# Matmul operand read as two half-rows in turn in a one-core decoder layer

## The chip, the core and the metric

One NeuronCore of a Trainium2 chip runs the whole kernel. The metric is the device time of one execution in microseconds (us), the median of the runs shown. The engines are named as in the profile: PE is TensorE, PEld its weight loads, DVE is VectorE, ACT is ScalarE, POOL is GpSimd, SP is SyncE, which issues most of the DMAs.

## The reference

The kernel computes one layer of a decoder for 256 prompt tokens and 32 sample tokens (8 sequences of 4), 2048 features wide, in float32. Cut to what matters here, with the attention and the convolutions named and not shown:

```python
z = einsum('ntd,de->nte', x, w_in)
h, gate_b, gate_c, q, k, v, g_a, g_b = split(z)
ya = gate_b * causal_conv3(gate_c * h)          # mixer A
yb = dilated_window_attention(q, k, v)          # mixer B, 3 groups of 4 heads
mixed = sigmoid(g_a) * (ya @ w_branch_a) + sigmoid(g_b) * (yb @ w_branch_b)
x1 = layernorm(ALPHA * x + mixed @ w_out)
a, b = split(x1 @ w_up)                         # 2048 -> 2 x 5632
y = layernorm(ALPHA * x1 + (silu(causal_conv3(a)) * b) @ w_down)
```

## The kernel before

Features lie on the 128 partitions and the T = 288 tokens (256 prompt, then 32 sample) lie along the free axis. An activation is a tile of KD = 16 rows per partition, one row of 288 float32 values for each block of 128 features. The activations of the layer's input stand in `xh` and `xl`; the other products read `yah`/`yal`, `ybh`/`ybl` (in later stages the names are reused for the mixed sum and the gated FFN values).

Every matrix product is made in float32r, a float32 form that PE takes in one pass, with three matmuls for one block of weights: each operand is split into a rounded high part and a low rest (`split`, `half_block`), and high times high, high times low and low times high are added up in PSUM. `mms` (lines 170 to 181) issues these three matmuls for each of the rows `k`: weights `hi[:, c, :]` (128x128) against the row `xh[:, k]`, the same weights against `xl[:, k]`, then `lo[:, c, :]` against `xh[:, k]`. A product over 16 rows is so 48 matmuls, each with its own weight load, into one PSUM tile `acc` of 288 columns; five such tiles are in use in turn.

`product` (line 157) takes the next prepared weights from `w_ready`, has `prepare` load (SP queue, tile `wst`, 1 MB) and split (ACT line 120, DVE line 121) the block after it, and calls `mms`. The stages follow each other: 12 products for q, 24 for k and v with the prompt's attention between them, 48 for mixer A, 64 for the two gated branches, 16 for `w_out`, then three parts of the FFN with 2 x 16, 2 x 16 and 2 x 12 products of `w_up`, each followed by 16 of `w_down`. The sample attention is woven in as steps between products of the early stages (its matmuls are lines 323 and 373).

In the first part of the FFN the normalisation is not applied to `x` before the product. Two columns more, the norm's scale and shift (`TG` = 290 columns), go through the same matmuls, and `normed` (line 581) puts the result right afterwards: it copies the two columns to a small tile `wgb` and corrects the 288 others with `n1.r` and `n1.nmr`. For this `xh` and `xl` have rows of `TX` = 296 values (1184 bytes); all other activations have rows of 288 (1152 bytes).

What leaves PSUM is read by ACT or DVE: `act.copy` of q, k, v and h, the sigmoids (lines 476, 487), `gated` (line 441), the products with `pc` (lines 461, 462), the sums into `dd` (lines 567, 573, 631, 635), `normed` (line 586) and the copies to `u` (lines 606, 607). POOL works on SBUF alone. The instruction order on each engine is the scheduler's, made when the program is built.

Of the kernel before, what the change touches and what calls it, by code (L numbers as in the profile page):

```python
# [11 lines left out]
F32R = mybir.dt.float32r  # L12
# [5 lines left out]
P = 128  # L18
# [4 lines left out]
NS = NB * NT  # L23
T = SEQ + NS

TG = T + 2
TX = T + 8
FF = 5632
KF = FF // P
HK = KD // 2  # L30
# [41 lines left out]
def layer_kernel(ctx: ExitStack, tc: tile.TileContext, ins, outs):  # L72
# [14 lines left out]
    def sb(pl, shape, tag, dt=F32, bufs=None):  # L87
        return pl.tile(shape, dt, tag=tag, name=nm(tag), bufs=bufs)

    def acc(cols=T):  # L90
        return sb(ps, [P, cols], "acc")

    def att(cols=512):
        return sb(ps, [P, cols], "att", bufs=2)
# [1 line left out]
    def f32(ap):  # L96
        return ap.bitcast(F32)
# [56 lines left out]
            copy_rest(d)  # L154
        w_ready.append([half_block(st, k0, min(HK, nk - k0)) for k0 in range(0, nk, HK)])

    def product(x, cols=T):

        w = w_ready.pop(0)
        if not w_ready:  # L160
            prepare()
        if steps_on[0]:
            spent[0] += N_STEP
            while spent[0] >= N_STEP_BLOCKS:
                spent[0] -= N_STEP_BLOCKS
                next(steps, None)
        o = acc(cols)
        mms(o, w, x)
        return o

    def mms(out, w, x):
        xh, xl = x
        nk = sum(n for _, _, n in w)
        k = 0
        for hi, lo, n in w:
            for c in range(n):
                n_cols = out.shape[-1]
                pe.matmul(out, hi[:, c, :], xh[:, k, :n_cols], start=k == 0, stop=False)  # L178
                pe.matmul(out, hi[:, c, :], xl[:, k, :n_cols], start=False, stop=False)  # L179
                pe.matmul(out, lo[:, c, :], xh[:, k, :n_cols], start=False, stop=k == nk - 1)  # L180
                k += 1

    def split(hi, lo, src):
        act.copy(hi, src)  # L184
        dve.tensor_tensor(lo, src, f32(hi), ALU.subtract)  # L185
# [4 lines left out]
    pool.memset(ones_p, 1.0 / P)  # L190


    xh = sb(big, [P, KD, TX], "xh", F32R)
    xl = sb(big, [P, KD, TX], "xl", F32R)
    x_in = ins["x"].rearrange("p (k t) -> p k t", t=T)
    xs = sb(big, [P, KD, T], "yah")
    w_ready = []
# [5 lines left out]
    for k0, n in FIRST:  # L203
        k = slice(k0, k0 + n)
        h = slice(k0 % HK, k0 % HK + n)
        for b, (st, src) in enumerate(stage):
            sp.dma_start(st[:, k, :], src[:, k, :])
            if b == 0:
                sp.dma_start(xs[:, k, :], x_in[:, k, :])
            hi, lo, _ = w_ready[b][k0 // HK]  # L210
            act.copy(hi[:, h, :], st[:, k, :])
            dve.tensor_tensor(lo[:, h, :], st[:, k, :], f32(hi[:, h, :]), ALU.subtract)
            if b == 0:
                split(xh[:, k, :T], xl[:, k, :T], xs[:, k, :])
    x = (xh, xl)

    cst = sb(big, [P, C_M0], "cst")

# [178 lines left out]
    kv = sb(big, [P, 2, 2, NG, T], "dd")  # L397
    for j in range(NH):
        for g in range(NG):
            act.copy(q_all[:, j, g], product(x))  # L400
            if j == 0 and g > 0:
                for dst, src in ((cst, ins["cst"][:, :C_M0]), (m_dist, ins["cst"][:, C_M0:])) if g == 1 else ((prm, ins["prm"]),):
                    behind(sp.dma_start(dst, src), w_load[0])
        pool.tensor_copy(q_s[:, :, j, :], q_all[:, j, :, SEQ:])
    steps_on[0] = True
    for j in range(NH):
        kT, vT = (kv[:, j % 2, c] for c in range(2))
        for g in range(NG):
            for t in (kT, vT):
                act.copy(t[:, g, :], product(x))  # L410
        pool.tensor_copy(k_s[:, :, j, :], kT[:, :, SEQ:])
        pool.tensor_copy(v_s[:, j], vT[:, :, SEQ:])
        act.dma_start(outs["o_k"][j].rearrange("p (g t) -> p g t", g=NG), kT)
        act.dma_start(outs["o_v"][j].rearrange("p (g t) -> p g t", g=NG), vT)
        prompt_attention(j, q_all[:, j], kT, vT)
# [16 lines left out]
    def samples(t):  # L432
        return t[:, SEQ:].rearrange("p (b r) -> p b r", b=NB)

    def last_rows(dst, u):
        pool.tensor_copy(dst[:, 0:2], u[:, SEQ : SEQ + 2])  # L436
        return pool.tensor_copy(
            dst[:, 2:].rearrange("p (b r) -> p b r", b=NB),
            u[:, SEQ + 2 :].rearrange("p (b r) -> p b r", b=NB)[:, :, NT:],
        )  # L440

    def gated(out, y, o, add=None):

        yt = y[:, SEQ : SEQ + NB * (NT + 2)].rearrange("p (b r) -> p b r", b=NB)
        for a, b, c in ((out[:, :SEQ], y[:, :SEQ], o[:, :SEQ]), (samples(out), yt[:, :, 2:], samples(o))):
            if add is None:
                dve.tensor_tensor(a, b, c, ALU.mult)  # L447
            else:
                dve.scalar_tensor_tensor(a, c, add, b, ALU.add, ALU.mult)

    yah = sb(big, [P, KD, T], "yah", F32R)
# [2 lines left out]
    for i in range(KD):  # L454
        ph = product(x)
        h = sb(wk, [P, T], "h", bufs=2)
        act.copy(h, ph)
        pc = product(x)
        u = sb(wk, [P, UW + 2], "u", bufs=2)
        up, us = conv_in(u[:, :UW], R_SM + i * 2 * NB)  # L460
        dve.tensor_tensor(up, h[:, :SEQ], pc[:, :SEQ], ALU.mult)  # L461
        dve.tensor_tensor(us, samples(h), samples(pc), ALU.mult)
        last_rows(cm[:, i], u[:, :UW])
        y = conv(u, R_WCM + i * 3)
        pb = product(x)
        ya = sb(wk, [P, T], "ya", bufs=2)
        gated(ya, y, pb)
        split(yah[:, i], yal[:, i], ya)
# [4 lines left out]
    for i in range(KD):  # L473
        pg = product(x)
        sg = sb(wk, [P, T], "h", bufs=2)
        act.activation(sg, pg, AF.Sigmoid)
        o = product((yah, yal))
        dve.tensor_tensor(ma[:, i], sg, o, ALU.mult)
    for _ in steps:
        pass  # L480
    steps_on[0] = False
# [2 lines left out]
    for i in range(KD):  # L484
        pg = product(x)
        sg = sb(wk, [P, T], "h", bufs=2)
        act.activation(sg, pg, AF.Sigmoid)
        o = product((ybh, ybl))
        m = sb(wk, [P, T], "ya", bufs=2)
        dve.tensor_tensor(m, sg, o, ALU.mult)  # L490
        pool.tensor_tensor(m, m, ma[:, i], ALU.add)  # L491
        split(mxh[:, i], mxl[:, i], m)

# [66 lines left out]

    n1 = Norm(R_LN, R_LN + KD)
    for i in range(KD):
        o = product((mxh, mxl))
        xf = sb(wk, [P, T], "h", bufs=2)
        pool.tensor_tensor(xf, f32(xh[:, i, :T]), f32(xl[:, i, :T]), ALU.add)
        if i == 0:
            dve.scalar_tensor_tensor(dd[:, i], xf, ALPHA, o, ALU.mult, ALU.add)
            n1.first()
            for c in range(2):
                split(xh[:, :, T + c], xl[:, :, T + c], prm[:, R_LN + c * KD : R_LN + (c + 1) * KD])  # L570
        else:
            dve.scalar_tensor_tensor(xf, xf, ALPHA, n1.c, ALU.mult, ALU.subtract)
            dve.tensor_tensor(dd[:, i], xf, o, ALU.add)  # L573
        act.activation(xh[:, i, :T], dd[:, i], AF.Copy, scale=n1.at(n1.g, i))
        dve.scalar_tensor_tensor(
            xl[:, i, :T], dd[:, i], n1.at(n1.g, i), f32(xh[:, i, :T]), ALU.mult, ALU.subtract
        )
        n1.add(i)
    n1.finish(False)

    def normed(o):

        w = sb(wk, [P, 2], "wgb", bufs=4)
        act.copy(w, o[:, T:])
        t = sb(wk, [P, T], "h", bufs=2)
        dve.tensor_tensor(t, o[:, :T], n1.r, ALU.mult)
        dve.scalar_tensor_tensor(t, n1.nmr, w[:, 0:1], t, ALU.mult, ALU.add)
        return t, w[:, 1:2]

# [4 lines left out]
    for part, nf in enumerate(THIRDS):  # L594
        gh = sb(big, [P, KD, T], "yah", F32R)
        gl = sb(big, [P, KD, T], "yal", F32R)
        for k in range(nf):
            pa = product(x, TG if part == 0 else T)
            u = sb(wk, [P, UW + 2], "u", bufs=2)
            up, us = conv_in(u[:, :UW], R_SF + f * 2 * NB)  # L600
            if part == 0:
                pa, b1 = normed(pa)
                act.activation(up, pa[:, :SEQ], AF.Identity, bias=b1)
                act.activation(us, samples(pa), AF.Identity, bias=b1)
            else:
                act.copy(up, pa[:, :SEQ])  # L606
                act.copy(us, samples(pa))
            i_rows = last_rows(cf[:, f], u[:, :UW])
            y = conv(u, R_WCF + f * 3)
            act.activation(y, y, AF.Silu)  # L610
            pb = product(x, TG if part == 0 else T)
            gf = sb(wk, [P, T], "ya", bufs=2)
            if part == 0:
                gated(gf, y, *normed(pb))
# [10 lines left out]
        if f == KF:  # L625
            sp.dma_start(outs["o_cf"].rearrange("p (k r) -> p k r", k=KF), cf)
        for i in range(KD):
            o = product((gh, gl))
            if part == 0:
                split(xh[:, i, :T], xl[:, i, :T], dd[:, i])  # L630
                dve.scalar_tensor_tensor(dd[:, i], dd[:, i], ALPHA, o, ALU.mult, ALU.add)
            else:
                if f == KF and i > 0:
                    pool.tensor_tensor(dd[:, i], dd[:, i], n2.c, ALU.subtract)
                dve.tensor_tensor(dd[:, i], dd[:, i], o, ALU.add)
            if f == KF:
                if i == 0:
                    n2.first()
                n2.add(i)
# [192 lines left out]
```

## Time and profile before

| what | value |
|---|---|
| median of 3 runs | 1914.95 us (1914.68 to 1915.04) |
| the profiled execution: its own time | 1915.33 us |
| its span in the trace | 1913.6 us |
| matmul records | 14257, of them 13632 in float32r into `acc` |
| granted PE clock, mean | 0.996 |
| DVE, ACT, POOL busy | 1009.6, 799.7, 257.6 us |
| HBM read, written | 389.89 MB, 94.53 MB |

The profile gives for each group of instructions the line, the engine, the tiles (out<-in), the shape, the count, the busy time and the mean length of one. Matmuls are pipelined: the length of one in the trace, some 0.3 us, runs past the start of the next. What counts for the time is the step from one start to the next, which is read from the timeline (start, length, what) or from a stretch of time divided by the number of matmuls in it (the windows: stretch, its length, then busy us and count for each engine).

### The profile page before, as it was taken

The numbers are of one execution on the slowest core, as the hardware profiler recorded it, in microseconds if no ns is written. First come the engines' busy times: TensorE is split into PE (matmuls) and PEld (weight loads), VectorE is DVE, ScalarE is ACT, GpSimd is POOL, SyncE is SP. The second block draws the span as 40 slices with busy tenths as digits, with TensorE's granted clock in tenths as the row PEclk, the third lists the DMA queues.
The fourth block names the chain that finished last, engine by engine and source line by source line (L and its number), as shares of the span: only waits on it lengthen the run. The fifth ranks groups of instructions, "written<-read, shape, count | busy, mean of one in ns | idle before, by whom it ended". The sixth has DMA issues, their size and how long they took to land.

```text
span 1913.6 us, 33492 instructions
## 1 busy us (share of the span) xinstructions
PE 1885.7 (99%) x14257; PEld 1848.0 (97%) x14257; DVE 1009.6 (53%) x1270; ACT 799.7 (42%) x1153; POOL 257.6 (13%) x406
## 2 busy tenths in 40 slices
PE   8999999999999999999999999999999999999995
PEld 8999999999999999999999999999999999999995
DVE  4444445445444433445587777764455554455555
ACT  4334443333333333344444555553444443344444
POOL 0000000000000000001154233310011100011174
PEclk9999999999999999999999999999999999999998
DMA  7586766777777777566755555556555555555552
GB/s 290 203 286 245 261 241 245 279 256 269 269 257 266 277 255 280 170 237 237 258 210 213 203 201 204 215 200 219 201 218 205 214 209 210 213 206 217 214 185 81
DMA packets 59862, 436.25 MB, mean 228 GB/s; under 512 B 7232, under 2 KB 7616, under 8 KB 15680
## 3 DMA queue, kind: packets, MB, share of 16 engines
q1 hardware_dynamic: 58560, 430.58, 62.3%
q10 hardware_dynamic: 1152, 3.54, 0.5%
q8 instruction: 111, 1.82, 0.4%
q14 instruction: 39, 0.32, 0.0%
HBM read 389.89 MB, written 94.53 MB: 253 GB/s over the span
## 4 chain that ended last, share of the span: by engine, by line
PE 98%; DVE 1%; ACT 0%; DMA 0%; ACTq 0%; SPq 0%; issue 0%
PE acc L178 32%; PE acc L180 32%; PE acc L179 31%; PE long L323 1%; PE long L373 1%; PE att L259 0%; PE att L278 0%; ACT yah L645 0%; DMA yah<-in_x 0%; DVE dd L543 0%; PE att L274 0%; DVE dd L557 0%; PE att L252 0%; PE att L529 0%; PE att L530 0%; DVE xl L185 0%
## 5 line engine op out<-in xcount | busy, mean ns | idle before, releaser
L121 DVE TENSOR_TENSOR wlo<-wst,whi 128x1024 fp32r<-128x1024 f32 (+1 forms) x580 | 706.3, 1219 | 713.6 <-ACT whi L120 700.8
L120 ACT CAST whi<-wst 128x1024 fp32r<-128x1024 f32 (+1 forms) x580 | 594.0, 1025 | 1004.0 <-PE acc L179 891.7
L178 PE MATMUL acc<-xh,whi 128*128 128x288 f32 (+1 forms) x3264 | 970.5, 298 | 7.4 <-ACT xh L184 7.4
L179 PE MATMUL acc<-xl,whi 128*128 128x288 f32 (+1 forms) x3264 | 966.8, 296 | 0.3 <-DVE xl L185 0.3
L180 PE MATMUL acc<-xh,wlo 128*128 128x288 f32 (+1 forms) x3264 | 967.1, 296 | 0.0
L178 PEld LDWEIGHTS acc<-xh,whi 128*128 128x128 f32 x3264 | 615.8, 189 | 28.1 <-issue 19.9
L180 PEld LDWEIGHTS acc<-xh,wlo 128*128 128x128 f32 x3264 | 616.2, 189 | 1.1 <-issue 0.8
L179 PEld LDWEIGHTS acc<-xl,whi 128*128 128x128 f32 x3264 | 615.6, 189 | 1.1 <-DVE xl L185 0.6
L180 PE MATMUL acc<-yah,wlo 128*128 128x288 f32 x1216 | 359.6, 296 | 0.0
L178 PE MATMUL acc<-yah,whi 128*128 128x288 f32 x1216 | 359.4, 296 | 0.0
L179 PE MATMUL acc<-yal,whi 128*128 128x288 f32 x1216 | 356.9, 294 | 0.0
L178 PEld LDWEIGHTS acc<-yah,whi 128*128 128x128 f32 x1216 | 228.6, 188 | 4.3 <-issue 4.2
L179 PEld LDWEIGHTS acc<-yal,whi 128*128 128x128 f32 x1216 | 228.6, 188 | 0.1
L180 PEld LDWEIGHTS acc<-yah,wlo 128*128 128x128 f32 x1216 | 228.3, 188 | 0.1
L436 POOL COPY qk_s<-u 128x2 f32<-128x2 f32 x44 | 43.5, 988 | 630.1 <-ACT u L606 480.4
L429 DVE SCALAR_TENSOR_TENSOR cy<-u,prm,cy 128x304 f32<-128x304 f32 x120 | 70.8, 590 | 3.1 <-ACT cy L427 0.3
L491 POOL TENSOR_TENSOR ya<-ya,dd 128x288 f32<-128x288 f32 x16 | 13.9, 868 | 332.8 <-DVE ya L490 332.8
L447 DVE TENSOR_TENSOR ya<-cy,acc 128x256 f32<-128x256 f32 x88 | 23.0, 301 | 44.1 <-PE acc L180 44.1
L436 POOL COPY cm<-u 128x2 f32<-128x2 f32 x16 | 3.0, 185 | 281.5 <-DVE u L461 281.5
L184 ACT CAST yah<-ya 128x288 fp32r<-128x288 f32 x76 | 32.7, 431 | 10.8 <-POOL ya L491 9.4
L185 DVE TENSOR_TENSOR yal<-ya,yah 128x288 fp32r<-128x288 f32 x76 | 35.0, 461 | 1.2 <-ACT yah L184 1.2
L521 POOL TENSOR_TENSOR cache<-cache,dd 128x288 f32<-128x288 f32 x28 | 26.8, 958 | 56.8 <-DVE dd L573 37.5
(146 smaller groups left out, 804.4 us busy)
## 6 DMA issues: line engine op xcount, KB each, us to landing
wst<-in_w_in SPq DMA_DIRECT2D x114, 1024.0 KB, 5.2
wst<-in_w_up SPq DMA_DIRECT2D x88, 1024.0 KB, 4.8
wst<-in_w_down SPq DMA_DIRECT2D x32, 1024.0 KB, 4.8
cache<-in_ck SPq DMA_DIRECT2D x18, 1024.0 KB, 6.9
out_o_ck<-cache SPq DMA_DIRECT2D x18, 1024.0 KB, 7.7
cache<-in_cv SPq DMA_DIRECT2D x18, 1024.0 KB, 7.0
out_o_cv<-cache SPq DMA_DIRECT2D x18, 1024.0 KB, 8.5
wst<-in_w_a SPq DMA_DIRECT2D x16, 1024.0 KB, 6.2
```

Source lines behind the costliest of these rows:

```text
L120: act.copy(hi[:, :n, :], st[:, k0 : k0 + n, :])
L121: dve.tensor_tensor(lo[:, :n, :], st[:, k0 : k0 + n, :], f32(hi[:, :n, :]), ALU.subtract)
L178: pe.matmul(out, hi[:, c, :], xh[:, k, :n_cols], start=k == 0, stop=False)
L179: pe.matmul(out, hi[:, c, :], xl[:, k, :n_cols], start=False, stop=False)
L180: pe.matmul(out, lo[:, c, :], xh[:, k, :n_cols], start=False, stop=k == nk - 1)
L184: act.copy(hi, src)
L185: dve.tensor_tensor(lo, src, f32(hi), ALU.subtract)
L323: pe.matmul(p[j * NS : (j + 1) * NS], qm[:, j, b, :], c[:, o + j * cols : o + (j + 1) * cols], start=b == 0, stop=b == NB - 1,)
L429: dve.scalar_tensor_tensor(y, u[:, i : i + YW], prm[:, w0 + i : w0 + i + 1], y, ALU.mult, ALU.add)
L436: pool.tensor_copy(dst[:, 0:2], u[:, SEQ : SEQ + 2])
L447: dve.tensor_tensor(a, b, c, ALU.mult)
L521: pool.tensor_tensor(self.s1, self.s1, d, ALU.add)
```

## The change

`xh` and `xl` get the shape [128, 16, 2, 160]: each row of 288 tokens is stored as two halves of 144 which start 160 values (640 bytes) apart, so a row takes 1280 bytes. The two columns for the norm become one more column in each half. The other activations keep their rows of 288 and are only seen as two halves of 144 (576 bytes apart).

The matmul reads its moving operand as column 0 of the first half, column 0 of the second, column 1 of the first, and so on. Its output is written in that order to consecutive PSUM columns, and whoever reads PSUM reads every second column to get a half back. Where the prompt's 256 columns were read alone they are now two pieces, 144 and 112, so that there are two instructions in place of one. The tile `wgb` gets two buffers in place of four. The core of the diff:

```diff
-TG = T + 2
-TX = T + 8
+H = T // 2
+HG = H + 1
+HX = 160
...
-    def acc(cols=T):
-        return sb(ps, [P, cols], "acc")
+    def acc(half=H):
+        return sb(ps, [P, half, 2], "acc")
+
+    def h2(ap):
+        return ap.rearrange("p (h a) -> p h a", h=2)
+
+    def h3(ap):
+        return ap.rearrange("p k (h a) -> p k h a", h=2)
...
-        o = acc(cols)
+        o = acc(x[0].shape[-1])
         mms(o, w, x)
-        return o
+        return o.rearrange("p a h -> p h a")
...
-                n_cols = out.shape[-1]
-                pe.matmul(out, hi[:, c, :], xh[:, k, :n_cols], start=k == 0, stop=False)
-                pe.matmul(out, hi[:, c, :], xl[:, k, :n_cols], start=False, stop=False)
-                pe.matmul(out, lo[:, c, :], xh[:, k, :n_cols], start=False, stop=k == nk - 1)
+                xh_k, xl_k = (t[:, k].rearrange("p h a -> p a h") for t in x)
+                pe.matmul(out, hi[:, c, :], xh_k, start=k == 0, stop=False)
+                pe.matmul(out, hi[:, c, :], xl_k, start=False, stop=False)
+                pe.matmul(out, lo[:, c, :], xh_k, start=False, stop=k == nk - 1)
...
-    xh = sb(big, [P, KD, TX], "xh", F32R)
-    xl = sb(big, [P, KD, TX], "xl", F32R)
+    xh = sb(big, [P, KD, 2, HX], "xh", F32R)
+    xl = sb(big, [P, KD, 2, HX], "xl", F32R)
...
-    x = (xh, xl)
+    x = (xh[:, :, :, :H], xl[:, :, :, :H])
+    x_gb = (xh[:, :, :, :HG], xl[:, :, :, :HG])
...
+    def pieces(up, us):
+
+        return up[:, :H], up[:, H:SEQ], us
+
+    def from_psum(o):
+        return o[:, 0], o[:, 1, : SEQ - H], o[:, 1, SEQ - H :].rearrange("p (b r) -> p b r", b=NB)
...
-        dve.tensor_tensor(up, h[:, :SEQ], pc[:, :SEQ], ALU.mult)
-        dve.tensor_tensor(us, samples(h), samples(pc), ALU.mult)
+        for a, b, c in zip(pieces(up, us), pieces(h, samples(h)), from_psum(pc)):
+            dve.tensor_tensor(a, b, c, ALU.mult)
...
-        o = product((yah, yal))
-        dve.tensor_tensor(ma[:, i], sg, o, ALU.mult)
+        o = product((h3(yah), h3(yal)))
+        dve.tensor_tensor(h2(ma[:, i]), h2(sg), o, ALU.mult)
...
-        w = sb(wk, [P, 2], "wgb", bufs=4)
-        act.copy(w, o[:, T:])
+        w = sb(wk, [P, 2], "wgb", bufs=2)
+        act.copy(w, o[:, :, H])
...
-                act.copy(up, pa[:, :SEQ])
-                act.copy(us, samples(pa))
+                for a, b in zip(pieces(up, us), from_psum(pa)):
+                    act.copy(a, b)
```

More of the change, by code (lines that the diff above doesn't have):

```diff
@@ L155, in prepare, with product @@
         w_ready.append([half_block(st, k0, min(HK, nk - k0)) for k0 in range(0, nk, HK)])
-    def product(x, cols=T):
+    def product(x):
         w = w_ready.pop(0)
@@ L166, in product @@
                 next(steps, None)
-        o = acc(cols)
+        o = acc(x[0].shape[-1])
         mms(o, w, x)
-        return o
+        return o.rearrange("p a h -> p h a")
     def mms(out, w, x):
-        xh, xl = x
         nk = sum(n for _, _, n in w)
@@ L213, in layer_kernel @@
             if b == 0:
-                split(xh[:, k, :T], xl[:, k, :T], xs[:, k, :])
-    x = (xh, xl)
+                split(xh[:, k, :, :H], xl[:, k, :, :H], h3(xs[:, k]))
+    x = (xh[:, :, :, :H], xl[:, :, :, :H])
+    x_gb = (xh[:, :, :, :HG], xl[:, :, :, :HG])
     cst = sb(big, [P, C_M0], "cst")
@@ L399, in layer_kernel @@
         for g in range(NG):
-            act.copy(q_all[:, j, g], product(x))
+            act.copy(h2(q_all[:, j, g]), product(x))
             if j == 0 and g > 0:
@@ L409, in layer_kernel @@
             for t in (kT, vT):
-                act.copy(t[:, g, :], product(x))
+                act.copy(h2(t[:, g, :]), product(x))
         pool.tensor_copy(k_s[:, :, j, :], kT[:, :, SEQ:])
@@ L444, in gated @@
         yt = y[:, SEQ : SEQ + NB * (NT + 2)].rearrange("p (b r) -> p b r", b=NB)
-        for a, b, c in ((out[:, :SEQ], y[:, :SEQ], o[:, :SEQ]), (samples(out), yt[:, :, 2:], samples(o))):
-            if add is None:
+        if add is None:
+            for a, b, c in zip(pieces(out, samples(out)), pieces(y, yt[:, :, 2:]), from_psum(o)):
                 dve.tensor_tensor(a, b, c, ALU.mult)
-            else:
+        else:
+            for a, b, c in ((out[:, :SEQ], y[:, :SEQ], o[:, :SEQ]), (samples(out), yt[:, :, 2:], samples(o))):
                 dve.scalar_tensor_tensor(a, c, add, b, ALU.add, ALU.mult)
@@ L456, in layer_kernel @@
         h = sb(wk, [P, T], "h", bufs=2)
-        act.copy(h, ph)
+        act.copy(h2(h), ph)
         pc = product(x)
@@ L475, in layer_kernel @@
         sg = sb(wk, [P, T], "h", bufs=2)
-        act.activation(sg, pg, AF.Sigmoid)
-        o = product((yah, yal))
-        dve.tensor_tensor(ma[:, i], sg, o, ALU.mult)
+        act.activation(h2(sg), pg, AF.Sigmoid)
+        o = product((h3(yah), h3(yal)))
+        dve.tensor_tensor(h2(ma[:, i]), h2(sg), o, ALU.mult)
     for _ in steps:
@@ L486, in layer_kernel @@
         sg = sb(wk, [P, T], "h", bufs=2)
-        act.activation(sg, pg, AF.Sigmoid)
-        o = product((ybh, ybl))
+        act.activation(h2(sg), pg, AF.Sigmoid)
+        o = product((h3(ybh), h3(ybl)))
         m = sb(wk, [P, T], "ya", bufs=2)
-        dve.tensor_tensor(m, sg, o, ALU.mult)
+        dve.tensor_tensor(h2(m), h2(sg), o, ALU.mult)
         pool.tensor_tensor(m, m, ma[:, i], ALU.add)
@@ L562, in layer_kernel @@
     for i in range(KD):
-        o = product((mxh, mxl))
+        o = product((h3(mxh), h3(mxl)))
         xf = sb(wk, [P, T], "h", bufs=2)
-        pool.tensor_tensor(xf, f32(xh[:, i, :T]), f32(xl[:, i, :T]), ALU.add)
+        pool.tensor_tensor(h2(xf), f32(x[0][:, i]), f32(x[1][:, i]), ALU.add)
         if i == 0:
-            dve.scalar_tensor_tensor(dd[:, i], xf, ALPHA, o, ALU.mult, ALU.add)
+            dve.scalar_tensor_tensor(h2(dd[:, i]), h2(xf), ALPHA, o, ALU.mult, ALU.add)
             n1.first()
             for c in range(2):
-                split(xh[:, :, T + c], xl[:, :, T + c], prm[:, R_LN + c * KD : R_LN + (c + 1) * KD])
+                split(xh[:, :, c, H], xl[:, :, c, H], prm[:, R_LN + c * KD : R_LN + (c + 1) * KD])
         else:
             dve.scalar_tensor_tensor(xf, xf, ALPHA, n1.c, ALU.mult, ALU.subtract)
-            dve.tensor_tensor(dd[:, i], xf, o, ALU.add)
-        act.activation(xh[:, i, :T], dd[:, i], AF.Copy, scale=n1.at(n1.g, i))
+            dve.tensor_tensor(h2(dd[:, i]), h2(xf), o, ALU.add)
+        act.activation(x[0][:, i], h2(dd[:, i]), AF.Copy, scale=n1.at(n1.g, i))
         dve.scalar_tensor_tensor(
-            xl[:, i, :T], dd[:, i], n1.at(n1.g, i), f32(xh[:, i, :T]), ALU.mult, ALU.subtract
+            x[1][:, i], h2(dd[:, i]), n1.at(n1.g, i), f32(x[0][:, i]), ALU.mult, ALU.subtract
         )
@@ L581, in normed @@
     def normed(o):
-        w = sb(wk, [P, 2], "wgb", bufs=4)
-        act.copy(w, o[:, T:])
+        w = sb(wk, [P, 2], "wgb", bufs=2)
+        act.copy(w, o[:, :, H])
         t = sb(wk, [P, T], "h", bufs=2)
-        dve.tensor_tensor(t, o[:, :T], n1.r, ALU.mult)
+        dve.tensor_tensor(h2(t), o[:, :, :H], h2(n1.r), ALU.mult)
         dve.scalar_tensor_tensor(t, n1.nmr, w[:, 0:1], t, ALU.mult, ALU.add)
@@ L597, in layer_kernel @@
         for k in range(nf):
-            pa = product(x, TG if part == 0 else T)
+            pa = product(x_gb if part == 0 else x)
             u = sb(wk, [P, UW + 2], "u", bufs=2)
@@ L610, in layer_kernel @@
             act.activation(y, y, AF.Silu)
-            pb = product(x, TG if part == 0 else T)
+            pb = product(x_gb if part == 0 else x)
             gf = sb(wk, [P, T], "ya", bufs=2)
@@ L627, in layer_kernel @@
         for i in range(KD):
-            o = product((gh, gl))
+            o = product((h3(gh), h3(gl)))
             if part == 0:
-                split(xh[:, i, :T], xl[:, i, :T], dd[:, i])
-                dve.scalar_tensor_tensor(dd[:, i], dd[:, i], ALPHA, o, ALU.mult, ALU.add)
+                split(x[0][:, i], x[1][:, i], h2(dd[:, i]))
+                dve.scalar_tensor_tensor(h2(dd[:, i]), h2(dd[:, i]), ALPHA, o, ALU.mult, ALU.add)
             else:
@@ L634, in layer_kernel @@
                     pool.tensor_tensor(dd[:, i], dd[:, i], n2.c, ALU.subtract)
-                dve.tensor_tensor(dd[:, i], dd[:, i], o, ALU.add)
+                dve.tensor_tensor(h2(dd[:, i]), h2(dd[:, i]), o, ALU.add)
             if f == KF:
```

## The prediction, made before the changed kernel ran

> **What bounds the kernel now.** I read the page first: the busy shares, the chain that ended last, and the granted clock.
>
> ```profile
> span 1913.6 us, 33492 instructions
> PE 1885.7 (99%) x14257; PEld 1848.0 (97%) x14257; DVE 1009.6 (53%) x1270; ACT 799.7 (42%) x1153; POOL 257.6 (13%) x406
> ...
> PEclk9999999999999999999999999999999999999998
> DMA  7586766777777777566755555556555555555552
> ...
> PE 98%; DVE 1%; ACT 0%; DMA 0%; ACTq 0%; SPq 0%; issue 0%
> ```
>
> PE is the bound from end to end: 98% of the chain is its own work, at full clock, and no other engine is busy for more than 53%. So the time is the number of matmuls times the step from one start to the next. Which matmuls, and how many, the groups by shape say (only the first of the three matmuls of a row is shown, line 178; lines 179 and 180 issue one each beside it).
>
> ```profile
> L178 PE MATMUL acc<-xh,whi 128*128 128x288 f32 x2752 | 817.7, 297 | 7.4 <-ACT xh L184 7.4
> L178 PE MATMUL acc<-yah,whi 128*128 128x288 f32 x1216 | 359.4, 296 | 0.0
> L178 PE MATMUL acc<-xh,whi 128*128 128x290 f32 x512 | 152.8, 298 | 0.0
> L178 PE MATMUL acc<-ybh,whi 128*128 128x288 f32 x64 | 18.8, 294 | 0.0
> ```
>
> Three times each: 8256 of 288 columns from xh/xl, 1536 of 290 columns from xh/xl, 3840 of 288 from the other activations; 13632 in all. The last column says that they wait once, 7.4 us at the very start. The mean length of one, 297 ns, overlaps the next; the step comes from windows that hold nothing but products.
>
> ```profile
> core 0: us, PE busy (x) PEld busy (x) DVE busy (x) ACT busy (x) POOL busy (x), PEclk, DMA share, GB/s
> 950.00:1058.00 108.00, 108.00 (x809) 107.47 (x808) 81.94 (x88) 51.75 (x74) 49.56 (x43) 1.00 0.57 210
> 1059.00:1148.00 89.00, 89.00 (x661) 89.00 (x661) 63.72 (x89) 47.61 (x85) 28.64 (x42) 1.00 0.58 213
> 1196.00:1244.00 48.00, 48.00 (x358) 48.00 (x357) 33.92 (x47) 24.25 (x43) 14.79 (x22) 1.00 0.57 214
> 1372.00:1560.00 188.00, 188.00 (x1424) 188.00 (x1423) 100.61 (x133) 85.50 (x133) 24.99 (x60) 1.00 0.58 211
> 1700.00:1820.00 120.00, 120.00 (x910) 120.00 (x909) 63.15 (x86) 54.39 (x85) 13.66 (x32) 1.00 0.59 214
> ```
>
> With 288 columns the step is 188/1424 = 132.0 and 120/910 = 131.9 ns; with 290 columns 89/661 = 134.6 and 48/358 = 134.1, say 134.4. Two columns cost 2.5 ns, though a column costs 132/288 = 0.46 on the mean. So a step isn't a fixed price plus a price per column. The timeline shows what else is in it.
>
> ```profile
> 1001.96 0.30 PE L178 MATMUL acc<-yah,whi 128*128 128x288 f32 x1
> 1002.10 0.29 PE L179 MATMUL acc<-yal,whi 128*128 128x288 f32 x1
> 1002.22 0.29 PE L180 MATMUL acc<-yah,wlo 128*128 128x288 f32 x1
> 1002.35 0.30 PE L178 MATMUL acc<-yah,whi 128*128 128x288 f32 x1
> 1002.49 0.30 PE L179 MATMUL acc<-yal,whi 128*128 128x288 f32 x1
> ...
> 1891.13 0.29 PE L180 MATMUL acc<-yah,wlo 128*128 128x288 f32 x1
> 1891.26 1.13 PE L529 MATMUL att<-cache,ones_d 128*128 128x288 f32 x4
> 1892.23 0.65 PE L530 MATMUL att<-dd,ones_d 128*128 128x288 f32 x2
> ```
>
> Matmuls of one shape, without a wait, step by 0.14, 0.12, 0.13, 0.14 us. What differs between them is where in the partition their operands lie. The norm's matmuls in plain float32 (L529, two passes for each of two matmuls, so x4) read as many columns at half the rate: (1892.23 - 1891.26)/4 = 242.5 ns, and half of that is 121.2. So the fast form stands 131.9 - 121.2 = 10.7 ns above twice the slow form's rate with 288 columns. With 290 the floor is 121.2 x 290/288 = 122.0, and the excess 12.4 ns.
>
> **The change, part by part.** *The read order.* Nothing is added to PE or taken from it: the same 13632 matmuls with as many columns. Only the order changes in which a row's columns are fetched; so the whole change is one number, what a step becomes. No row of before reads the moving operand in any order but ascending, so I bound it. From below: the floor, 121.2 and 122.0 ns. From above: one column at a time at the slow form's rate, 242.5 ns, which is a rival below. In the new order each of the two streams advances one column in two PE beats, the pace at which the plain float32 pass goes through its row, and that pass shows no excess. If the excess is the moving read running into the weight load of the next matmul (PEld is 97% busy, so a weight load is always beside it), two streams at half the pace should give most of it back. I take the floor for the products on xh/xl, since there every row begins at the same place (1280 bytes a row, 640 between the halves), and leave the other activations at 131.9, since their halves lie 576 bytes apart and their rows alternate as now.
>
> Sum: 8256 x 10.7 ns = 88.3 us; 1536 x 12.4 ns = 19.0 us; together 107.3 us off PE's time.
>
> *The way out.* The pieces add 44 DVE instructions in `gated`, 16 for mixer A's `u` and 28 ACT copies of the FFN's `u`; these rows price them.
>
> ```profile
> L606 ACT COPY u<-acc 128x256 f32<-128x256 f32 x28 | 10.3, 366 | 0.0
> L607 ACT COPY u<-acc 128x32 f32<-128x32 f32 x28 | 5.3, 191 | 0.0
> L461 DVE TENSOR_TENSOR u<-h,acc 128x256 f32<-128x256 f32 x16 | 6.8, 423 | 18.5 <-PE acc L180 18.5
> L462 DVE TENSOR_TENSOR u<-h,acc 128x32 f32<-128x32 f32 x16 | 2.9, 182 | 0.0
> L586 DVE TENSOR_TENSOR h<-acc,cache 128x288 f32<-128x288 f32 x32 | 14.3, 448 | 0.0
> L573 DVE TENSOR_TENSOR dd<-h,acc 128x288 f32<-128x288 f32 x15 | 6.8, 453 | 10.5 <-PE acc L180 10.5
> ```
>
> DVE: (423 - 182)/224 = 1.08 ns a column, so 182 - 32 x 1.08 = 148 ns fixed, and 60 x 148 = 8.9 us. ACT: (366 - 191)/224 = 0.78, so 166 ns fixed, 28 x 166 = 4.6 us. Both lie under PE. Reading every second PSUM column has no row: at best it costs nothing, at worst, I assume, it doubles an eviction, 448 ns. In the FFN's first part two L586 fall on a pair of products (96 x 134.4 = 12.9 us): 0.9 us, so DVE goes from 63.72/89 = 72% to 79%, and to 87% at the quicker step. In the `w_out` stage it goes from 81.94/108 = 76% by one L573 in 48 x 131.9 = 6.3 us to 83%, and to 90%. Still under PE. An eviction that is 0.45 us later delays no product, since five accumulators stand for five products of 6.3 us; if that cover were gone, each of the 300 products could lose 0.45 us, 135 us in all. At the end only the last sum into `dd` is exposed: at most 0.5 us, which I add.
>
> *Loads.* Weights land well ahead of use:
>
> ```profile
> wst<-in_w_in SPq DMA_DIRECT2D x114, 1024.0 KB, 5.2
> ```
>
> A product of 48 steps at 121.2 ns still takes 5.8 us, and the DMA row's busiest slices (8 tenths) leave room for steps 8% shorter. The order of instructions on SP and POOL is unchanged. The smaller `wgb` pool matters for two products in flight, which is what the loop keeps.
>
> The profiled execution took 1915.33 us, 0.38 over the median of the runs. 1915.3 - 107.3 + 0.5 = 1808.5; against the median **1808 us**. If the other activations gain too, 3840 x 10.7 = 41.1 us more: 1767. If xh/xl give back half: 1862. The forecast's own range is 1765 to 1870.
>
> **The rivals.** *A, the double step (slower).* If PE's read is quick only because neighbours come together, then taking a column from each half in turn leaves each fetch one useful value, and the step becomes the slow form's: 288 columns in 242.5 ns, 290 in 244.2. Price: 12096 x (242.5 - 131.9) + 1536 x (244.2 - 134.4) = 1337.8 + 168.7 = 1506.5 us, so **3422 us**; with the present excess kept on top, 146 us more. It decides from the first product on, at any spacing of the halves. For it: the slow and the fast form differ by just this factor, and every read of before is ascending. Against it: in before nothing reads out of order, so no row shows that order matters to that degree. [...]
>
> *B, the stalls double.* Two streams meet the weight load twice as often as one, each time at today's price: the excess goes from 10.7 to 21.4 and from 12.4 to 24.8 ns: 12096 x 10.7 + 1536 x 12.4 = 148.5 us, **2064 us**. For it: steps already differ by 0.02 us with the place. Against it: the slow form, which meets the weight load for twice as long, has no excess to show.
>
> *C, it doesn't do what it says.* The excess belongs to the change of weights, not to the read: the step stays, the evictions stay hidden, **1915 us** plus at most 0.5. Against it: the 2.5 ns for two columns, and the different steps of one shape.
>
> **How the numbers follow.** Forecast, with its variants of 1767 and 1862: 0.62. A 0.20, B 0.14, C 0.04. The time is the likeliest case's, 1808. The range 1760 to 2080 holds the forecast, C and B, 0.80, and leaves out A. Faster by over 0.2% (3.8 us, about what the measurement can tell from no change): 0.62; within 0.2%: 0.04; slower: A and B, 0.34.
>
> **What would show it.** Windows in the FFN's later parts (288 columns from xh/xl) with steps near 121 ns, and of the same length one after the other, show the floor right; `w_down` windows near 132 show the other activations as I left them, near 121 the variant of 1767. Steps near 242 are A, near 143 B, at 132 C. On the way out, L586's successor at 450 ns or up to 900 tells the price of the strided PSUM read, and idle time of PE ahead of line 178's matmuls, released by DVE or ACT, would show that it wasn't hidden. The forecast is wrong if the step doesn't fall on xh/xl.

## The result, and the profile after

The changed kernel takes 1778.15 us (median of 4 runs, 1777.65 to 1779.09) where the kernel before takes 1914.82 beside it: a ratio of 0.9287, 95% interval 0.9271 to 0.9303. The forecast was 1808, with 1767 as its variant.

The page of the changed kernel, with the lines that answer to those of before:

```profile
span 1776.2 us, 33581 instructions
...
PE 1748.1 (98%) x14257; PEld 1710.9 (96%) x14257; DVE 1015.4 (57%) x1330; ACT 801.8 (45%) x1181; POOL 255.2 (14%) x406
...
PEclk9999999999999999999999999999999999999998
DMA  8587776878778878567766566656666666666552
...
PE 97%; ACT 1%; DVE 1%; POOL 0%; DMA 0%; issue 0%; ACTq 0%; SPq 0%
```

As many matmuls as before, at the same clock (0.995, 0.996 before), and PE is still the bound; the span is 137.4 us shorter. The windows (stretch, length, then busy us and count for PE, PEld, DVE, ACT, POOL, clock, DMA share, GB/s) lie inside, in this order, `w_up` of the FFN's part one (290 columns), `w_down` of part one, `w_up` and `w_down` of part two, `w_up` of part three:

```profile
980.00:1160.00 180.00, 180.00 (x1462) 180.00 (x1461) 143.73 (x201) 106.99 (x186) 60.68 (x90) 1.00 0.61 223
...
1178.00:1258.00 80.00, 80.00 (x656) 80.00 (x655) 41.89 (x46) 30.14 (x29) 0.00 (x0) 1.00 0.66 240
...
1265.00:1445.00 180.00, 180.00 (x1472) 180.00 (x1471) 104.58 (x153) 89.93 (x156) 25.46 (x62) 1.00 0.63 225
1452.00:1537.00 85.00, 85.00 (x696) 85.00 (x695) 42.09 (x45) 30.34 (x29) 0.00 (x0) 1.00 0.64 234
1550.00:1674.00 124.00, 124.00 (x1014) 124.00 (x1013) 72.69 (x108) 61.25 (x104) 16.53 (x42) 1.00 0.62 225
```

The step with 288 columns is 180/1472 and 124/1014 = 122.3 ns on xh/xl and 80/656 = 122.0, 85/696 = 122.1 on the other activations; with 290 columns it is 180/1462 = 123.1. The kernel before, in `w_down` of part one, shows what the other activations came from, 92/698 = 131.8 ns:

```profile
1262.00:1354.00 92.00, 92.00 (x698) 92.00 (x697) 45.47 (x51) 32.94 (x34) 0.73 (x3) 1.00 0.59 217
```

Against 132.0 and 134.4 before, 12096 x 9.7 + 1536 x 11.3 = 117.3 + 17.4 = 134.7 us: nearly all of the 137.4. A window also counts the one to three matmuls that only reach into it, so a step read from it is up to 0.9 ns low. By the starts of all matmuls of a stage, without those next to a wait or another kind of matmul, the steps are 132.2 and 135.0 ns before, 122.5 and 123.3 after. The steps have also become even, as consecutive matmuls of the timeline (start, length) show:

```profile
1399.85 0.29 PE L185 MATMUL acc<-xh,whi 128*128 128x288 f32 x1
1399.97 0.29 PE L186 MATMUL acc<-xl,whi 128*128 128x288 f32 x1
1400.09 0.29 PE L187 MATMUL acc<-xh,wlo 128*128 128x288 f32 x1
1400.22 0.29 PE L185 MATMUL acc<-xh,whi 128*128 128x288 f32 x1
1400.34 0.29 PE L186 MATMUL acc<-xl,whi 128*128 128x288 f32 x1
```

The groups on the way out (mean ns of one after the busy time):

```profile
L602 DVE TENSOR_TENSOR h<-acc,cache 128x288 f32<-128x288 f32 x32 | 14.3, 448 | 0.0
L589 DVE TENSOR_TENSOR dd<-h,acc 128x288 f32<-128x288 f32 x15 | 6.8, 452 | 4.2 <-PE acc L187 4.2
L185 PE MATMUL acc<-yah,whi 128*128 128x288 f32 x1216 | 348.4, 287 | 0.4 <-ACT yah L191 0.4
```

For DVE, reading every second PSUM column costs what reading them in a row did (448 ns before as after). The only new wait of PE on an eviction's successor is 0.4 us in the whole run.

### The profile page after: what moved, and what is told of

It reads as the page before. It is cut to its first block, busy times and chain, and to the rows that moved or that the text cites. A ratio compares the mean times of both kernels' runs of the same rounds, so it can differ in the third digit from the quotient of the medians.

```text
span 1776.2 us, 33581 instructions
## 1 busy us (share of the span) xinstructions
PE 1748.1 (98%) x14257; PEld 1710.9 (96%) x14257; DVE 1015.4 (57%) x1330; ACT 801.8 (45%) x1181; POOL 255.2 (14%) x406
## 4 chain that ended last, share of the span: by engine, by line
PE 97%; ACT 1%; DVE 1%; POOL 0%; DMA 0%; issue 0%; ACTq 0%; SPq 0%
PE acc L185 31%; PE acc L187 31%; PE acc L186 31%; PE long L331 1%; PE long L381 1%; PE att L267 0%; PE att L286 0%; ACT yah L661 0%; ACT xh L191 0%; DMA yah<-in_x 0%; POOL qk_s L451 0%; DVE dd L559 0%; PE att L282 0%; ACT whi L128 0%; DVE dd L573 0%; PE att L260 0%
## 5 line engine op out<-in xcount | busy, mean ns | idle before, releaser
L185 PE MATMUL acc<-xh,whi 128*128 128x288 f32 (+1 forms) x3264 | 940.7, 288 | 7.2 <-ACT xh L191 7.2
L186 PE MATMUL acc<-xl,whi 128*128 128x288 f32 (+1 forms) x3264 | 936.5, 287 | 0.3 <-DVE xl L192 0.3
L187 PE MATMUL acc<-xh,wlo 128*128 128x288 f32 (+1 forms) x3264 | 936.4, 287 | 0.0
L185 PE MATMUL acc<-yah,whi 128*128 128x288 f32 x1216 | 348.4, 287 | 0.4 <-ACT yah L191 0.4
L187 PE MATMUL acc<-yah,wlo 128*128 128x288 f32 x1216 | 347.8, 286 | 0.0
L186 PE MATMUL acc<-yal,whi 128*128 128x288 f32 x1216 | 347.6, 286 | 0.0
L462 DVE TENSOR_TENSOR ya<-cy,acc 128x144 f32<-128x144 f32 x132 | 25.7, 249 | 33.4 <-PE acc L187 33.4
L435 ACT ACTIVATE cy<-u,prm 128x304 f32<-128x304 f32 x60 | 32.9, 548 | 3.2
```

Of the source, the lines that this page charges most:

```text
L185: pe.matmul(out, hi[:, c, :], xh_k, start=k == 0, stop=False)
L186: pe.matmul(out, hi[:, c, :], xl_k, start=False, stop=False)
L187: pe.matmul(out, lo[:, c, :], xh_k, start=False, stop=k == nk - 1)
L435: act.activation(y, u[:, :YW], AF.Copy, scale=prm[:, w0 : w0 + 1])
```

## The experiments

Experiments 1 to 6 change how the matmuls of `mms` read, so each diff is cut to that. All steps below are a window's length divided by its matmuls, unless the text says otherwise. Experiments 1 to 6 ran once each.

**1. Layout without the order.**

```diff
-                xh_k, xl_k = (t[:, k].rearrange("p h a -> p a h") for t in x)
+                xh_k, xl_k = (t[:, k] for t in x)
```

The PSUM tile is [128, 2, half] to match, and each half of the norm's part has 146 columns in place of 145.

> The changed kernel's layout (halves 640 bytes apart, rows of 1280 bytes, all rows beginning at one place) with each half read ascending, one after the other; only the taking in turn is undone. The norm's part has 292 columns instead of 290. Theory 'in turn' (a read that goes up through its row at full pace is slowed, two streams in turn are not): the step is back at 131 to 134 ns, time 1905 to 1925 us. Rival 'layout' (the row's starts and the gap between the halves took the stalls away): the step stays at 122.5 ns on xh/xl, time 1775 to 1820 us.

Measured: 1906.94 us, beside 1914.63 for the kernel before. `w_up` of parts two and three:

```profile
1355.00:1550.00 195.00, 195.00 (x1483) 195.00 (x1483) 106.11 (x154) 89.96 (x157) 25.19 (x62) 1.00 0.57 210
1660.00:1800.00 140.00, 140.00 (x1065) 140.00 (x1064) 75.28 (x111) 64.49 (x111) 17.50 (x42) 1.00 0.56 209
```

195/1483 = 131.5 and 140/1065 = 131.5 ns. Padding and row starts are worth half a nanosecond at most; the order is the change.

**2. Is it the weight load?** The forecast's reason was that the read runs into the weight load of the next matmul. Here the columns that it loads are cut to a half and a quarter.

```diff
-                pe.matmul(out, hi[:, c, :], xl[:, k, :n_cols], start=False, stop=False)
+                pe.matmul(out[:m], hi[:, c, :m], xl[:, k, :n_cols], start=False, stop=False)
```

The same for the other two, with `m` 64 in part two and 32 in part three.

> The kernel before, but in the FFN's parts two and three the weights of all matmuls but the first and the last of a product have 64 columns (part two) or 32 columns (part three); the sums of the other output rows are left out, so the result differs there. The moving read is as before. Theory 'weight load' (the excess comes from the read meeting the weight load of the next matmul): the excess over 122.5 ns shrinks with the columns, to some 127 ns a step in part two and 125 or less in part three. Rival 'own read' (the ascending read slows itself): 131 to 134 ns in all parts.

Measured: 1911.55 us, beside 1914.63 for the kernel before. The windows are `w_up` of part two, then `w_up` of part three; below them the weight loads, first of the kernel before (128 columns), then of these two stages (64 and 32 columns):

```profile
1362.00:1554.00 192.00, 192.00 (x1460) 191.82 (x1459) 102.10 (x137) 88.19 (x138) 25.04 (x60) 1.00 0.57 212
...
1664.00:1808.00 144.00, 144.00 (x1097) 119.61 (x1096) 77.47 (x103) 65.49 (x105) 18.66 (x44) 1.00 0.56 207
...
L179 PEld LDWEIGHTS acc<-xl,whi 128*128 128x128 f32 x3264 | 615.6, 189 | 1.1 <-DVE xl L185 0.6 <-issue 0.2
L183 PEld LDWEIGHTS acc<-xl,whi 128*64 128x64 f32 x487 | 65.2, 134 | 0.1
L183 PEld LDWEIGHTS acc<-xl,whi 128*32 128x32 f32 x365 | 39.4, 108 | 8.1
```

131.5 and 131.3 ns, against 132.0 and 131.9 in the same stages before, though PEld is busy for only 119.61 of 144 us in the second. By its record a load of half the columns isn't half as long: 134 ns, and 108 with a quarter, in place of 189. If the excess of some 9.7 ns went with that length, the steps would still have come down to about 129 and 128 ns; they came down by 0.5 and 0.6. So the length of the load isn't the reason. That a load of any length costs the 9.7 ns is ruled out by experiment 3, where loads of all 128 columns stand beside steps of 122 ns: the forecast's reason falls.

**3. Does the distance between the streams matter?** Rows as before, the operand given by hand as 144 steps of 1 over 2 steps of the distance; `VAR[0]` holds the stage's distance, `T // 2` is 144.

```diff
+        r = t[:, k, :]
+        return bass.AP(r.tensor, r.offset, [list(r.ap[0]), [1, T // 2], [VAR[0], 2]])
...
-                pe.matmul(out, hi[:, c, :], xh[:, k, :n_cols], start=k == 0, stop=False)
+                xh_k, xl_k = (moving(t, k, n_cols) for t in (xh, xl))
+                pe.matmul(out, hi[:, c, :], xh_k, start=k == 0, stop=False)
```

> The kernel before, but from the first w_down on the moving operand is taken from two streams of 144 whose distance is a number of values: 1 in w_down of part one, 16 in w_up of part two, 4 in w_down of part two, 64 in w_up of part three, 128 in w_down of part three. Streams overlap, so the products from there on are of other columns than the reference's. Theory 'weight load': half the pace through the row is what counts, so 122.5 ns at every distance. Rival 'own read' (two accesses in a row to one place cost, far apart they don't): 132 ns or more at distances 1 and 4, perhaps 16, and 122.5 at 64 and 128. [...]

Measured: 1867.91 us. Distances 1, 16, 4, 64, 128 in order of time:

```profile
1260.00:1345.00 85.00, 85.00 (x695) 84.99 (x695) 45.49 (x53) 32.74 (x34) 1.87 (x4) 1.00 0.65 235
1355.00:1530.00 175.00, 175.00 (x1431) 175.00 (x1431) 100.50 (x135) 86.81 (x135) 24.98 (x60) 1.00 0.63 226
1542.00:1628.00 86.00, 86.00 (x705) 86.00 (x704) 43.10 (x45) 30.34 (x29) 0.00 (x0) 1.00 0.62 231
1636.00:1768.00 132.00, 132.00 (x1079) 132.00 (x1079) 75.85 (x101) 64.61 (x102) 18.14 (x43) 1.00 0.62 225
1778.00:1840.00 62.00, 62.00 (x506) 61.90 (x506) 36.18 (x44) 27.17 (x41) 43.56 (x42) 1.00 0.46 158
```

122.3, 122.3, 122.0, 122.3 and 122.5 ns (by the matmuls' starts 122.5 in all five): no distance matters, not even 1, where the order is 0, 1, 1, 2, 2, 3. So it isn't two places far apart that help, either. The rival that hung on distance, 'own read', missed. The theory 'weight load' had the numbers right, half the pace through the row is enough, but experiment 2 had taken its reason away.

**4. One stream that skips.**

```diff
+        r = t[:, min(k, rows - step), :]
+        return bass.AP(r.tensor, r.offset, [list(r.ap[0]), [step, T]])
```

> The kernel before with rows of 290 values, and from the first w_down on one stream of 288 values that takes every 2nd value (w_down of part one), every 4th (w_up and w_down of part two), every 8th (w_up of part three), every 2nd (w_down of part three), running on into the next rows; the products from there on are of other values than the reference's. Theory 'weight load': a read that passes the weight load quicker meets it more often for a shorter time, so the step stays within 122 to 135 ns at every stride. Rival 'own read': the step falls to 122.5 when neighbours are no longer taken in a row. [...]

Measured: 2514.16 us. Every 2nd, 4th and 8th value (`w_down` of part one, `w_up` of part two, `w_up` of part three):

```profile
1265.00:1450.00 185.00, 185.00 (x723) 149.91 (x722) 46.97 (x54) 33.03 (x34) 2.14 (x6) 1.00 0.31 110
1465.00:1850.00 385.00, 385.00 (x1475) 307.22 (x1474) 104.91 (x139) 88.77 (x139) 26.49 (x64) 1.00 0.29 104
...
2065.00:2335.00 270.00, 270.00 (x1104) 225.98 (x1103) 77.47 (x103) 66.69 (x105) 18.65 (x44) 1.00 0.30 111
```

255.9, 261.0 and 244.6 ns. 'Weight load' and 'own read' miss. This is near the double step of the forecast's rival A (242.5 ns), in a read that it wasn't named for, and it begins at every 2nd value already.

All the steps so far sort by one count on the order of the columns. Take columns 0, 2, 4, ... of a matmul by themselves and columns 1, 3, 5, ... by themselves, cut the row into groups of four values, and count how often each of the two sequences enters another group. Two streams in turn enter 36 groups and step in 122.0 to 122.5 ns; an ascending row enters 72, at 132.0; a step of 2 or more 144, at 244.6 to 261.0. Of groups of two, four and eight only four fits: by twos an ascending row would count 144 like every 2nd value, though they step in 132.0 and 255.9 ns; by eights every 2nd value would count 72 and every 4th 144, though they step in 255.9 and 261.0. This sorts the measured steps and no more; no record shows how the columns are fetched. The next two kernels were built to break it.

**5 and 6. Other orders.** The same edit with other steps; rows of 290 values in `xh`/`xl`. By the count, and from the steps so far, I estimated, in the order of the expectations' lists, 256, 132, 180 to 256, 256 and 132 ns for `e5_pairs`, and 122.5, 122.5, some 132 and 256 for `e6_more`. In `e6_more` the expectation misdescribes one stage: `w_up` of part three read four streams of 72 in the order 0, 144, 72, 216, 1, and only `w_down` of part three the pairs from each half.

> The kernel before with rows of 290 values, and from the first w_down on other orders of the moving read, so that the products from there on are of other values than the reference's: four streams of 72 in turn (w_down of part one), four neighbours taken and four skipped (w_up of part two), pairs of neighbours that begin 3 values apart (w_down of part two), pairs of neighbours that begin 4 values apart (w_up of part three), two streams 16 apart that each take every 2nd value (w_down of part three). [...] Rival 'inner pair' (the form with a short inner run is quick whatever it reads): 122.5 in all five.

> As e5_pairs, with these orders: two streams 143 apart (w_down of part one), each value twice (w_up of part two), runs of four that take every 2nd value and begin 4 apart (w_down of part two), pairs of neighbours from each half in turn (w_up of part three: 0, 1, 144, 145, 2, 3, ...; w_down of part three is the same order). [...] Rival 'inner pair': 122.5 in all.

Measured: 2209.08 and 1956.31 us. Of the first, four streams, pairs 3 apart, pairs 4 apart, and two streams 16 apart that take every 2nd value:

```profile
1265.00:1372.00 107.00, 107.00 (x697) 107.00 (x696) 45.68 (x53) 32.15 (x34) 2.25 (x6) 1.00 0.50 187
...
1672.00:1810.00 138.00, 138.00 (x718) 138.00 (x717) 43.58 (x45) 30.49 (x31) 0.00 (x0) 1.00 0.39 142
1820.00:2105.00 285.00, 285.00 (x1111) 229.98 (x1110) 77.47 (x103) 67.30 (x106) 18.68 (x44) 1.00 0.30 110
2115.00:2180.00 65.00, 65.00 (x507) 64.89 (x506) 35.45 (x43) 28.18 (x42) 43.60 (x42) 1.00 0.44 152
```

Of the second, each value twice, runs of four, four streams in the other order, and pairs from each half:

```profile
1360.00:1540.00 180.00, 180.00 (x1470) 180.00 (x1469) 103.29 (x138) 88.74 (x139) 26.18 (x62) 1.00 0.62 226
1550.00:1640.00 90.00, 90.00 (x674) 90.00 (x673) 40.69 (x43) 29.44 (x29) 0.00 (x0) 1.00 0.57 211
1650.00:1820.00 170.00, 170.00 (x1101) 170.00 (x1100) 77.43 (x103) 66.30 (x105) 18.66 (x44) 1.00 0.47 176
1830.00:1928.00 98.00, 98.00 (x527) 97.89 (x526) 35.20 (x44) 30.32 (x44) 41.78 (x44) 1.00 0.29 100
```

All orders but one together, with the number of groups (to within one) that every second column, 144 values, enters:

| order of the columns | groups entered | step, ns |
|---|---|---|
| two streams, distance 1 to 160 | 36 | 122.0 to 122.5 |
| each value twice | 36 | 122.4 |
| ascending (before; experiment 1) | 72 | 132.0; 131.5 |
| two streams 16 apart, every 2nd value of each | 72 | 128.2 |
| runs of four every 2nd value, 4 apart | 72 | 133.5 |
| pairs of neighbours 3 apart | 108 | 192.2 |
| pairs of neighbours 4 apart | 144 | 256.5 |
| one stream, every 2nd / 4th / 8th | 144 | 255.9 / 261.0 / 244.6 |
| four streams of 72, two orders | 144, to and fro between two | 153.5; 154.4 |
| pairs from each half in turn | 144, to and fro between two | 186.0 |

256.5/144 = 1.78 ns and 192.2/108 = 1.78 ns a group. As an estimate from these two rows, 72 groups come to 128 ns, just over the 122 ns of the quick orders, and 36 to 64 ns, well under it. Pairs 4 apart are the sharpest row: both neighbours come from one group, one right after the other, and at 256.5 ns it is as slow as one stream that skips. With that row the rival 'inner pair' (122.5) falls, and so does any account by which two neighbours in a row from one group are enough. Nor is it the number of groups in a matmul as a whole: an ascending row and its two halves in turn hold the same 72 groups, at 131.8 and 122.0 ns (`w_down` of part one, before and after). The count isn't the whole price: the three strides have 144 each and spread from 244.6 to 261.0 ns.

The four neighbours taken and four skipped gave a mixture, 278 us for 1487 matmuls or 187.0 ns where I expected 132, which the timeline of experiment 5 resolves: rows there lie 290 values apart, so they begin by turns on a group and two values into one (taking the tile to begin on a group).

```profile
1499.59 0.43 PE L189 MATMUL acc<-xh,whi 128*128 128x288 f32 x1
1499.84 0.44 PE L190 MATMUL acc<-xl,whi 128*128 128x288 f32 x1
1500.10 0.44 PE L191 MATMUL acc<-xh,wlo 128*128 128x288 f32 x1
1500.36 0.31 PE L189 MATMUL acc<-xh,whi 128*128 128x288 f32 x1
1500.51 0.29 PE L190 MATMUL acc<-xl,whi 128*128 128x288 f32 x1
1500.64 0.29 PE L191 MATMUL acc<-xh,wlo 128*128 128x288 f32 x1
1500.77 0.42 PE L189 MATMUL acc<-xh,whi 128*128 128x288 f32 x1
```

One row's three matmuls step by about 0.26 us, the next row's by about 0.13. Where the four neighbours are one group, the count is 72, where they straddle two, 144: the two steps of the trace go with it, near the 132.0 and 256 ns of the other rows with 72 and 144.

Four streams and the pairs from each half missed what I expected (256): 154 and 186. There every second column goes to and fro between two groups in place of on to new ones. Why that costs less was not tested, so the count stands for the other orders and is open for these.

**7. Halves at an odd place.**

```diff
-HX = 160
+HX = 146
```

> The changed kernel with halves 146 values apart (584 bytes, no multiple of 16) in place of 160, which gives back 3.5 KB of each partition, and four wgb buffers again. [...]

I estimated 122.5 ns and 1777 to 1780 us if it doesn't matter where the halves begin, and 125 to 133 ns and 1800 to 1880 us if it does.

Measured over 4 runs: 1778.46 us, ratio 0.9288 (0.9273 to 0.9304), `w_up` of part two:

```profile
1265.00:1445.00 180.00, 180.00 (x1471) 180.00 (x1471) 104.38 (x152) 89.75 (x155) 24.79 (x61) 1.00 0.62 227
```

180/1471 = 122.4 ns, as in the changed kernel (122.3): halves that begin 584 bytes apart in place of 640 cost nothing. The 160 isn't needed; it costs 3.5 KB a partition for nothing. No version tried is quicker than the changed kernel.

## Why the prediction was right, and where not

*The bound and the form of the answer* held: nothing but the step changed, PE stayed the bound, and the direction and most of the size followed from the excess over twice the slow form's rate.

*The floor* was put too low, 121.2 against 122.3 measured with 288 columns, 122.0 against 123.1 with 290. I halved the whole step of the plain float32 pass, 242.5 ns. A part of it doesn't halve, by this estimate: if the columns take c in the fast form and 2c in the slow one, and both have the same rest, then 242.5 - 122.3 = 120.2 ns is c and 2.1 ns is the rest. On 9792 matmuls that is 9792 x 1.1 = 11 us less gain than written.

*The other activations* are the step that failed. I left 3840 matmuls at 131.9 ns because their halves lie 576 bytes apart and their rows alternate; they went to 122.1, 3840 x 9.8 = 38 us more. Experiments 3 and 7 show that neither distance nor row start plays a part in two streams. The forecast's variant (1767) had them gain but with the floor too low; both corrected give a gain of 107.3 - 11 + 38 = 134 us, so 1782; the 3 us to the 137.4 are no more than the windows' reading error on 13632 steps.

*The reason* was wrong though the sum came near, and that is in part luck: two errors of opposite sign, 11 and 38 us, stand in the sum. The read doesn't lose its time to the weight load (experiments 2 and 3). What the runs show in its place is the count that sorts most of the orders: an ascending row enters 72 groups, at an estimated 1.78 ns each 128 ns, more than the 122.3 measured for the changed order, which enters 36. Half the pace was the right thing to ask for. That the plain float32 pass "shows no excess" was no reading when I wrote it, since the excess was counted from that pass itself; now it is one, for 242.5 is no more than twice 122.3.

*Rival A*'s condition, that the read is quick only because neighbours come together, isn't borne out: no neighbours follow each other in the changed kernel, and it steps in 122.0 to 122.3 ns with 288 columns. Its double step came in other orders alone, 244.6 to 261.0 ns with one stream that skips and 256.5 with pairs 4 apart. The 146 us that rival A adds for the present excess should be 148.5, as under rival B. *B* and *C* found nothing: no step at 143 or 132 is left.

*The way out* was as forecast: hidden. The pieces themselves cost what was forecast: DVE's in `gated` and `u` went from 36.2 to 45.0 us (8.8 more, 8.9 forecast), ACT's for `u` from 15.6 to 20.4 (4.8, 4.6 forecast). In all, DVE grew by 5.8 us and ACT by 2.1. The strided PSUM read cost nothing on DVE (448 ns before and after) or on ACT (the copies to `dd` 391 ns before and after), and the 0.45 us for it stayed a bound. Of the forecast's windows the first, 950 to 1058, isn't products alone: it runs 10 us into the FFN and holds the norm's matmuls; only DVE's 76% rests on it, which is 75.19/96 = 78% where the stage is alone (950 to 1046). The busiest DMA slices stay at 8 tenths, and PE shows no wait for a load.

## What to carry to other kernels

Where matmuls in a one-pass float32 form set the time, compare their step with half that of a plain float32 matmul of as many columns (here 132.0 with 121.2); if it stands some nanoseconds above and varies with the row, look at the order of the moving read. Let columns 0, 2, 4, ... and columns 1, 3, 5, ... each walk through consecutive values (here 122.0 to 122.5 ns), and undo the order in PSUM, where strided reads were free here (448 ns on DVE and 391 on ACT, before and after). Don't read such a row as one stream that skips: every second value already doubled the step (255.9 ns), while two streams in turn that each took every second value stepped in 128.2 ns.

## What the runs showed of the hardware that I had not expected

Two streams one value apart, which read nearly every value twice, step in 122.3 ns, while the plain ascending row takes 132.0. Cutting the weight load to 32 columns changes the step of an ascending read by some 0.6 ns. Why an ascending row takes some 4 ns more than the 128 ns estimated for its 72 groups, and why by an amount that varies from row to row (steps of 0.12 to 0.14 us in the forecast's timeline), was not tried and stays open.
